# Longer priority leads for the loads, and stores issued from ACT's queue, in a hybrid gMLP, SSD and PEER block on one core

## The chip, the core and the metric

The kernel runs on one core of a Trainium2 chip. The metric is device time in microseconds (us) from launch to end; the table below gives the runs of the kernel before the change and one profiled execution of it. A core has five engines with an instruction queue each, which run in parallel and each in order: TensorE (PE, matmuls; its weight loads are listed as PEld), VectorE (DVE), ScalarE (ACT), GpSimd (POOL) and SyncE (SP, which here does nothing but issue DMA transfers). An instruction that waits for a semaphore holds everything behind it on its own queue.

## The reference

One block over 1024 tokens of width 1024, all in float32. It has three parts.

```python
uv, z, xbc, dt_raw, gate_pre = split(x @ w_in)          # 10272 columns
ya = gmlp_branch(uv, ...) @ gm_w_out                    # gelu, layer norm, causal mixing in chunks of 128
yb = ssd_branch(z, xbc, dt_raw, ...) @ ssd_w_out        # conv, chunked state-space scan, 32 heads
merged = gates[0] * ya + gates[1] * yb
x1 = layer_norm(ALPHA * x + merged @ w_o)
# PEER: 8 heads, each picks 16 of 16384 experts per token
q = x1 @ w_q;  s1, s2 = q . k1, q . k2;  top-16 of each, then top-16 of their sums -> experts, gates
act = gelu(sum_d u[experts] * x1);  ch = sum_k gates * act * v[experts]
ple = sigmoid(x1 @ ple_w_gate + b) * (p @ ple_w_proj)
out = layer_norm(ALPHA * x1 + ch + ple)
```

## The kernel before

The tokens are cut into three groups of 256, 384 and 384 (`GROUPS`). For each, `front` runs the dense layers of the block: gMLP (`w_v`, `w_u`, then eight pairs of `w_g` and `gm_w_out`), SSD (16 pairs of heads `j`, each with `make_x`, `core_g`, `core`), the merge, `w_o`, and the query and key products (`w_q`, `kT`). The experts of the first two groups are gathered row by row from DRAM by POOL (`gather`, 4 KB per partition), multiplied on DVE (`row`, L822) and PE (`pacc`, L864). This side work is spread over the later groups' `front` by the loop at the end of the kernel. The third group instead multiplies by all 16384 experts: `dense_scores` and `dense_gates` prepare 48 of 128 score tiles (`s_d`) and the gate table (`g_d`) in DRAM, then `dense` runs 16 steps of 8 pieces. A piece of a step either loads its score tile (`ew<-s`) or makes it on PE (`ew<-mm` by ACT), multiplies it with a gate tile (`gte`, one load of 12 by 128 stretches per partition for four pieces) and splits it in two; `po` then takes 768 by 3 matmuls of it, and `eacc` adds `po` into the result. Six of the 16 steps load their pieces; they are called the loading steps here.

Every weight goes through `weights`: a load into `raw` (4 buffers), a cast to `whi` on ACT (3 buffers), and the rest `wlo` on DVE (3 buffers). PE multiplies high by high, high by low and low by high.

A scheduler orders the program. It takes instructions by priority, which is the order in which they were written unless `tc.high_priority(offset=n)` moves one n places ahead, and it places a load once its buffer is free in its own account of the program. The queues are then fixed: SP issues its DMAs in that order, whether or not a later one could go. Before the change SP issues every load of weights and activations and nearly every store; ACT issues none. The stores wait on SP for what they store.

The lines that matter: L144 issues `raw`, L146 and L147 make `whi` and `wlo`; L348 stores `m0`, L440 loads the state of the group before into `pv`, L452 stores the new state, L486 stores `yacc`; L571 stores `x1` for the gathers; L590 loads `kT`; L917 and L952 store the scores `s` and gates `g`; L975 and L980 load `gte` and `ew`; L1013 is the `eacc` addition.

Of the kernel before, what the change touches and what calls it, by code (L numbers as in the profile page):

```python
# [8 lines left out]
F32 = mybir.dt.float32  # L9
# [13 lines left out]
NG = len(GROUPS)  # L23
# [3 lines left out]
NCOL = 32  # L27
# [13 lines left out]
CST = 300  # L41
AHEAD_W = (20, 20)
AHEAD_G = 40
LEAD = 50
# [34 lines left out]
def block_kernel(ctx, tc, a, out):  # L79
# [135 lines left out]
    def front(gi):  # L215
        NB, mode = GROUPS[gi]
# [23 lines left out]
        with tc.tile_pool(name="ga", bufs=1, side=side_) as ga, \  # L240
# [17 lines left out]
            with tc.tile_pool(name="sd", bufs=1, side=side_) as sd:  # L258
# [50 lines left out]
                for c in range(NB):  # L309
                    DMA.dma_start(arow[:, c, :], act[c * NCOL:(c + 1) * NCOL, :])  # L310

# [11 lines left out]
            for g in range(8):  # L323
# [15 lines left out]
                yield 1.2 * unit  # L339
            m0 = []  # L340
            for j in range(8):
                pg = channel_major(a["w_g"][j], xh, xl)
                sg = gb.tile([128, T], F32, name="sg", tag="t1", bufs=3)
                A.activation(sg, pg, AF.Sigmoid, bias=bgate[:, j:j + 1])
                py = channel_major(a["gm_w_out"][j], gh, gl)
                V.tensor_mul(sg, sg, py)
                m0.append(dram.tile([128, T], F32, name=f"m0_{gi}_{j}"))
                DMA.dma_start(m0[j], sg)  # L348
                beside()
                yield 2 * unit  # L350

        for _ in previous:
# [5 lines left out]
        yacc = []  # L358
# [5 lines left out]
        with tc.tile_pool(name="sa", bufs=1, side=side_) as sa, tc.tile_pool(name="sb", bufs=2, side=side_) as sb:  # L364
# [17 lines left out]

            bT, cT, xs, zs, arows, btok, cbm = [{} for _ in range(7)]

# [6 lines left out]
            def make_x(j):  # L391
                arows[j] = sb.tile([128, 2, T], F32, name="arow_t")
                DMA.dma_start(arows[j], bass.AP(tensor=arow.tensor, offset=arow.offset + 2 * j * T,
                                                ap=[[0, 128], [T, 2], [1, T]]))
                xs[j] = conv(channel_major(a["w_xbc"][j], xh, xl), j, "xs")
                yield unit
                zp = channel_major(a["w_z"][j], xh, xl)
                zs[j] = sb.tile([128, T], F32, name="zs")
                A.activation(zs[j], zp, AF.Silu)
                yield unit  # L400
# [14 lines left out]
            def core(j):  # L415
# [22 lines left out]
                pv = sa.tile([128, NB, 2, 64], F32, name="pv")  # L438
                if gi > 0:
                    DMA.dma_start(pv[:, 0], state_d[gi - 1, j])  # L440

                for c in range(NB if gi < NG - 1 else NB - 1):
                    if c + gi == 0:
                        A.copy(pv[:, 1], pst_[:, 0])
                        continue
                    for h in range(2):
                        V.scalar_tensor_tensor(pv[:, (c + 1) % NB, h], pv[:, c, h],
                                               cdec[:, c, 2 * j + h:2 * j + h + 1], pst_[:, c, h],
                                               op0=OP.mult, op1=OP.add)
                if gi < NG - 1:  # L450
                    state_d[gi, j] = dram.tile([128, 2, 64], F32, name=f"state_{gi}_{j}")
                    DMA.dma_start(state_d[gi, j], pv[:, 0])  # L452
                V.tensor_mul(dec, dec, cbm[g].unsqueeze(1).to_broadcast([128, 2, NB, 128]))
# [4 lines left out]
                for c in range(NB):  # L458
                    for h in range(2):
                        o = py[h * 64:h * 64 + 64, c, :]  # L460
                        PE.matmul(o, lhsT=xdt[:, c, h, :], rhs=dec[:, h, c, :], start=True, stop=(c + gi == 0),
                                  tile_position=(0, h * 64))
                        if c + gi > 0:
                            PE.matmul(o, lhsT=pv[:, c, h, :], rhs=ce[:, h, c * 128:c * 128 + 128],
                                      start=False, stop=True, tile_position=(0, h * 64))
# [4 lines left out]
                sq = rrow if j == 0 else sa.tile([128, T], F32, name="sq")  # L470
                A.activation(sq, y, AF.Square)
                if j > 0:
                    V.tensor_add(rrow, rrow, sq)
# [6 lines left out]
            def first_half():  # L480
                for j in range(8):
                    p = channel_major(a["ssd_w_out"][j, 0], yfh, yfl)
                    o = sb.tile([128, T], F32, name="yo")
                    A.copy(o, p)
                    yacc.append(dram.tile([128, T], F32, name=f"yacc_{gi}_{j}"))
                    DMA.dma_start(yacc[j], o)  # L486
                    yield unit
# [73 lines left out]
        with tc.tile_pool(name="qa", bufs=1, side=side_) as qa, tc.tile_pool(name="qb", bufs=2, side=side_) as qb:  # L561

            for c in range(NB):
                mv = qb.tile([128, 2], F32, name="mv")
                V.bn_aggr(mv, st[:, c])
                rs = rstd_of(mv[:, 1:2], 1, qb)
                V.scalar_tensor_tensor(x1[:, c], x1[:, c], mv[:, 0:1], lg, op0=OP.subtract, op1=OP.mult)
                V.scalar_tensor_tensor(x1[:, c], x1[:, c], rs, lb, op0=OP.mult, op1=OP.add)
                if mode == "gather":
                    x1_d[gi, c] = dram.tile([128, 1024], F32, name=f"x1_{gi}_{c}")  # L570
                    DMA.dma_start(x1_d[gi, c], x1[:, c])  # L571
            for u in range(4):
                for cc, p in token_major([a["ple_w_proj"][u]], ph, pl, 2):
                    A.copy(proj[:, cc, u * 256:u * 256 + 256], p)
                yield 0.5 * unit
            for c in range(NB):
                for k4 in range(2):
                    pt = pst.tile([128, 4, 128], F32, name="mt", tag="mt")
                    for k in range(4):
                        kk = 4 * k4 + k  # L580
                        PE.transpose(pt[:, k, :], x1[:, c, kk * 128:kk * 128 + 128], ident)
                    sl = (slice(None), slice(4 * k4, 4 * k4 + 4), slice(c * 128, c * 128 + 128))
                    split(xh[sl], xl[sl], pt)
# [3 lines left out]
            for u in range(16):  # L587
                p = channel_major(a["w_q"][u], xh, xl)
                kT = qb.tile([128, 128], F32, name="kT", bufs=3)
                DMA.dma_start(kT, a["kT"][:, u, :])  # L590
                qT = qb.tile([128, T], F32, name="qT")
# [318 lines left out]
    def dense_scores(gi, xh, xl, pool):  # L910

        for i2 in range(sum(AHEAD)):
# [3 lines left out]
            s_d[gi, i2] = dram.tile([128, xh.shape[2]], F32, name=f"s_{gi}_{i2}")  # L916
            DMA.dma_start(s_d[gi, i2], w)  # L917
            yield UNIT * xh.shape[2] / 512

    def dense_gates(gi, NB, pst):  # L920
        with tc.tile_pool(name="da", bufs=1) as da, tc.tile_pool(name="db", bufs=3) as db:
# [9 lines left out]
            for c in range(T // TC):  # L931
# [19 lines left out]
                for b in range(0, 128 * TC, 2048):  # L951
                    DMA.dma_start(g_d[gi][c, :, b:b + 2048], gf[:, b:b + 2048])  # L952

    def dense(gi, t0, NB, xh, xl):
        T = NB * 128
        with tc.tile_pool(name="ea", bufs=1) as ea, tc.tile_pool(name="eb", bufs=2) as eb, \
# [35 lines left out]
            for step, b in enumerate(order):  # L992
# [3 lines left out]
                for h in range(2):  # L996
# [14 lines left out]
                    for c in range(NB):  # L1011
                        o = acc[:, c, h * 512:h * 512 + 512]
                        V.tensor_add(o, o, po[c])  # L1013
                        if last:
                            V.bn_stats(st[:, c, h, :], o)
# [104 lines left out]
```

## Time and profile before

| | |
|---|---|
| median of 3 runs | 3764.52 us (3756.73 to 3765.45) |
| the profiled execution | 3774.55 us, of which 3772.9 us is the span from the first to the last instruction |
| busy, share of the span | PE 91%, PEld 78%, DVE 78%, ACT 47%, POOL 43% |
| moved by DMA | 1183.88 MB, mean 314 GB/s |
| mean granted PE clock | 0.955 of full speed |

The profiled execution is 10.0 us longer than the median of the runs. An idle figure in a row stands for the time just before the instructions named, and the name behind the arrow is what ended the wait. SP counts no busy time: its rows tell when it issued a DMA and how long that took. A load's time of flight is the time from its issue to its landing.

### The profile page before, as it was taken

The numbers are of one execution on the slowest core, as the hardware profiler recorded it, in microseconds if no ns is written. First come the engines' busy times: TensorE is split into PE (matmuls) and PEld (weight loads), VectorE is DVE, ScalarE is ACT, GpSimd is POOL, SyncE is SP. The second block draws the span as 40 slices with busy tenths as digits, with TensorE's granted clock in tenths as the row PEclk, the third lists the DMA queues.
The fourth block names the chain that finished last, engine by engine and source line by source line (L and its number), as shares of the span: only waits on it lengthen the run. The fifth ranks groups of instructions, "written<-read, shape, count | busy, mean of one in ns | idle before, by whom it ended". The sixth has DMA issues, their size and how long they took to land.

```text
span 3772.9 us, 59493 instructions
## 1 busy us (share of the span) xinstructions
PE 3437.7 (91%) x21390; PEld 2946.2 (78%) x21390; DVE 2936.8 (78%) x6823; ACT 1756.0 (47%) x2675; POOL 1606.3 (43%) x1310
## 2 busy tenths in 40 slices
PE   8898997999989988999988989998889989989988
PEld 8897996988877876888878888777667868667756
DVE  6677799898977989896688999997667766766535
ACT  6788543476843333466652334774222323322223
POOL 0000004756545354554354445443556565665540
PEclk9998998999999988999989999999999999999999
DMA  5453656989879886989888899999999999999992
GB/s 200 161 172 130 238 180 241 389 309 356 317 279 385 309 324 234 356 311 343 305 326 327 298 338 349 362 377 372 360 381 400 395 386 389 368 383 401 356 350 95
DMA packets 409159, 1183.88 MB, mean 314 GB/s; under 512 B 41120, under 2 KB 139424, under 8 KB 405792
## 3 DMA queue, kind: packets, MB, share of 16 engines
q0 software_dynamic: 187488, 682.71, 47.7%
q1 hardware_dynamic: 221376, 497.38, 36.9%
q8 instruction: 168, 2.75, 0.3%
q14 instruction: 127, 1.04, 0.1%
HBM read 1121.01 MB, written 58.92 MB: 313 GB/s over the span
## 4 chain that ended last, share of the span: by engine, by line
PE 33%; DVE 16%; DMA 13%; issue 4%; ACT 1%; POOL 1%; SPq 0%; DVEq 0%; ACTq 0%; POOLq 0%
PE mm L152 6%; PE mm L154 6%; PE mm L153 6%; PE pacc L864 4%; DVE row L822 3%; DVE wlo L147 3%; DMA ew<-s 3%; PE po L152 3%; DMA row<-in_peer_v_dram,idxT 3%; PE po L153 3%; PE po L154 3%; DMA raw<-in_peer_uT_dram 2%; PE mt L947 2%; DMA row<-in_peer_u_dram,idx 1%; DMA raw<-in_peer_vd_dram 1%
## 5 line engine op out<-in xcount | busy, mean ns | idle before, releaser
L146 ACT CAST whi<-raw 128x1024 fp32r<-128x1024 f32 (+1 forms) x676 | 701.1, 1041 | 1192.4 <-PE mm L153 612.0
L803 POOL DMA_INDIRECT row<-in_peer_u_dram,idx x640 | 811.5, 1268 | 874.9 <-PE pacc L864 254.3
L147 DVE TENSOR_TENSOR wlo<-raw,whi 128x1024 fp32r<-128x1024 f32 (+1 forms) x676 | 816.2, 1210 | 375.5 <-ACT whi L146 374.7
L154 PE MATMUL mm<-xh,wlo 128*128 128x384 f32 (+2 forms) x3160 | 1056.4, 335 | 46.7 <-DVE wlo L147 46.7
L152 PE MATMUL mm<-xh,whi 128*128 128x384 f32 (+2 forms) x3160 | 1066.3, 338 | 34.3 <-ACT whi L146 25.6
L803 POOL DMA_INDIRECT row<-in_peer_v_dram,idxT x640 | 780.9, 1220 | 712.0 <-PE pacc L864 232.5
L153 PE MATMUL mm<-xl,whi 128*128 128x384 f32 (+2 forms) x3160 | 1051.9, 333 | 0.6 <-DVE xl L136 0.6
L822 DVE SCALAR_TENSOR_TENSOR row<-row,x1b 128x1024 f32<-128x1024 f32 x640 | 774.6, 1217 | 64.8 <-DMA row<-in_peer_u_dram,idx 58.5
L152 PEld LDWEIGHTS mm<-xh,whi 128*128 128x128 f32 (+1 forms) x3160 | 611.2, 194 | 89.7 <-ACT whi L146 46.1
L154 PEld LDWEIGHTS mm<-xh,wlo 128*128 128x128 f32 (+1 forms) x3160 | 609.8, 193 | 66.4 <-DVE wlo L147 55.0
L153 PEld LDWEIGHTS mm<-xl,whi 128*128 128x128 f32 (+1 forms) x3160 | 610.5, 193 | 12.2 <-issue 6.1
L864 PE MATMUL pacc<-row,zw 128*32 128x512 f32 x2560 | 316.9, 614 | 37.0 <-DMA row<-in_peer_v_dram,idxT 36.8
L152 PE MATMUL po<-whi,ewh 128*128 128x512 f32 x768 | 316.0, 411 | 32.2 <-DVE eacc L1013 32.2
L153 PE MATMUL po<-wlo,ewh 128*128 128x512 f32 x768 | 311.0, 405 | 14.4 <-DVE wlo L147 14.3
L154 PE MATMUL po<-whi,ewl 128*128 128x512 f32 x768 | 309.9, 404 | 0.0
L152 PEld LDWEIGHTS po<-whi,ewh 128*128 128x128 f32 x768 | 148.3, 193 | 104.6 <-DVE eacc L1013 36.1
L864 PEld LDWEIGHTS pacc<-row,zw 128*32 128x32 f32 x2560 | 67.9, 111 | 180.6 <-issue 131.1
L135 ACT CAST ewh<-ew 128x384 fp32r<-128x384 f32 x128 | 65.6, 514 | 296.7 <-DVE ew L985 230.1
L818 POOL DMA_DIRECT2D x1b<-x x5 | 3.0, 601 | 446.4 <-DMA x<-x 446.4
L153 PEld LDWEIGHTS po<-wlo,ewh 128*128 128x128 f32 x768 | 148.5, 193 | 51.0 <-DVE wlo L147 16.8
L154 PEld LDWEIGHTS po<-whi,ewl 128*128 128x128 f32 x768 | 148.1, 193 | 40.9 <-issue 5.0
L153 PE MATMUL mm<-wlo,xh 128*128 128x256 f32 x512 | 147.8, 289 | 11.4 <-DVE wlo L147 11.4
(272 smaller groups left out, 5603.8 us busy)
## 6 DMA issues: line engine op xcount, KB each, us to landing
raw<-in_peer_uT_dram SPq DMA_DIRECT2D x128, 512.0 KB, 8.0
raw<-in_peer_vd_dram SPq DMA_DIRECT2D x128, 512.0 KB, 6.8
raw<-in_w_xbc_dram SPq DMA_DIRECT2D x96, 512.0 KB, 5.9
raw<-in_w_g_dram SPq DMA_DIRECT2D x48, 512.0 KB, 6.7
raw<-in_w_z_dram SPq DMA_DIRECT2D x48, 512.0 KB, 5.4
raw<-in_ssd_w_out_dram SPq DMA_DIRECT2D x48, 512.0 KB, 5.3
raw<-in_w_q_dram SPq DMA_DIRECT2D x48, 512.0 KB, 4.7
g<-gt SPq DMA_DIRECT2D x24, 1024.0 KB, 7.5
```

The lines of the kernel that those rows point to most:

```text
L135: A.copy(hi, src)
L146: A.copy(hi, raw)
L147: V.tensor_sub(lo, raw, hi.bitcast(F32))
L152: PE.matmul(p, lhsT=lh, rhs=rh, start=start, stop=False, skip_group_check=skip)
L153: PE.matmul(p, lhsT=lh, rhs=rl, start=False, stop=False, skip_group_check=skip)
L154: PE.matmul(p, lhsT=ll, rhs=rh, start=False, stop=stop, skip_group_check=skip)
L803: g = POOL.indirect_dma_start(out=t, out_offset=None, in_=a[tab], in_offset=bass.IndirectOffsetOnAxis(ap=ix, axis=0))
L818: POOL.dma_start(x1, x1_d[gi, c])
L822: u = V.scalar_tensor_tensor(t, t, 1.0, x1, op0=OP.mult, op1=OP.mult, accum_out=act[:, k:k + 1])
L864: return PE.matmul(pacc[q * 32:q * 32 + 32, h * 512:h * 512 + 512], lhsT=zws[z][:, q, r % 4, :], rhs=ts[q][:, h * 512:h * 512 + 512], star ...
L947: PE.matmul(p[:, i, :], lhsT=o1, rhs=o2, start=True, stop=True)
```

## The change

Priorities: a weight's load goes from 20 to 150 places ahead (`AHEAD_W[0]`), the dense group's `gte` and `ew` loads from 40 to 300 (`AHEAD_G`), and the `eacc` addition, which had no offset, gets 60 (`AHEAD_E`). The `kT` load becomes one of two tiles and gets the weights' 150. Stores: `arow`, `m0`, `state`, `yacc`, `x1`, `s` and `g` go to ACT's queue, 157 DMAs in all; `m0` is issued one turn later than its product, `state` after the square of `y`, `x1` after the `ple_w_proj` products. The state of the group before is loaded into a tile of its own (`p0`, 2 buffers) in `make_x`, ahead of its use. Buffers stay as they are, apart from `p0` and `kT`.

```diff
-AHEAD_W = (20, 20)
-AHEAD_G = 40
+AHEAD_W = (150, 20)
+AHEAD_G, AHEAD_E = 300, 60
...
-                    DMA.dma_start(arow[:, c, :], act[c * NCOL:(c + 1) * NCOL, :])
+                    A.dma_start(arow[:, c, :], act[c * NCOL:(c + 1) * NCOL, :])
...
                 A.activation(sg, pg, AF.Sigmoid, bias=bgate[:, j:j + 1])
+                if late:
+                    A.dma_start(*late.pop())
                 py = channel_major(a["gm_w_out"][j], gh, gl)
                 V.tensor_mul(sg, sg, py)
                 m0.append(dram.tile([128, T], F32, name=f"m0_{gi}_{j}"))
-                DMA.dma_start(m0[j], sg)
+                late.append((m0[j], sg))
...
+                if gi > 0:
+                    pvs[j] = sb.tile([128, 2, 64], F32, name="p0")
+                    DMA.dma_start(pvs[j], state_d[gi - 1, j])
                 xs[j] = conv(channel_major(a["w_xbc"][j], xh, xl), j, "xs")
...
-                if gi > 0:
-                    DMA.dma_start(pv[:, 0], state_d[gi - 1, j])
+                p0 = pvs.pop(j, None)
...
-                    DMA.dma_start(state_d[gi, j], pv[:, 0])
...
                 A.activation(sq, y, AF.Square)
+                if gi < NG - 1:
+                    A.dma_start(state_d[gi, j], pv[:, 0])
...
-                    DMA.dma_start(yacc[j], o)
+                    A.dma_start(yacc[j], o)
...
-                    DMA.dma_start(x1_d[gi, c], x1[:, c])
+                    A.dma_start(x1_d[gi, c], x1[:, c])
...
-                kT = qb.tile([128, 128], F32, name="kT", bufs=3)
-                DMA.dma_start(kT, a["kT"][:, u, :])
+                if u % 2 == 0:
+                    k2 = qb.tile([128, 2, 128], F32, name="kT")
+                    with tc.high_priority(offset=AHEAD_W[0]):
+                        DMA.dma_start(k2, a["kT"][:, u:u + 2, :])
...
-            DMA.dma_start(s_d[gi, i2], w)
+            A.dma_start(s_d[gi, i2], w)
...
-                    DMA.dma_start(g_d[gi][c, :, b:b + 2048], gf[:, b:b + 2048])
+                    A.dma_start(g_d[gi][c, :, b:b + 2048], gf[:, b:b + 2048])
...
-                        V.tensor_add(o, o, po[c])
+                        with tc.high_priority(offset=AHEAD_E):
+                            V.tensor_add(o, o, po[c])
```

What the scheduler makes of it is seen in the queues. First SP at the end of the score and gate stage (`raw<-in_peer_uT` are the weights, `s` and `sah` the score stores, `eacc<-base` and `gte` the first loads of `dense`), before:

```order
L144 DMA raw<-in_peer_uT_dram 128x1024 x2
L917 DMA s_44_28235<-sah 128x384
L962 DMA eacc<-base_23083 128x1024
L917 DMA s_45_28284<-sah 128x384
L962 DMA eacc<-base_23083 128x1024 x2
L144 DMA raw<-in_peer_uT_dram 128x1024
L917 DMA s_46_28324<-sah 128x384
L144 DMA raw<-in_peer_uT_dram 128x1024 x2
L917 DMA s_47_28364<-sah 128x384
L144 DMA raw<-in_peer_uT_dram 128x1024 x2
L975 DMA gte<-g_24888 128x12x128 x2
```

The same place of SP after the change:

```order
L144 DMA raw<-in_peer_uT_dram 128x1024 x3
L761 DMA sel_2_24683<-sT 128x384
L144 DMA raw<-in_peer_uT_dram 128x1024
L938 DMA sT<-sel_2_24683 128x3x128
L144 DMA raw<-in_peer_uT_dram 128x1024 x28
L144 DMA raw<-in_peer_vd_dram 128x1024
L985 DMA gte<-g_24872 128x12x128 x2
L972 DMA eacc<-base_23067 128x1024 x3
```

The stores are gone from between the weights, which now stand in an unbroken row of 28, and the `eacc` loads have moved behind the first `gte`.

Second, SP in a loading step of `dense`, the one that loads the score tiles 8 to 15 (`ew<-s_2_8` to `s_2_15`; the number behind a tile's name is that of its creation), before:

```order
L980 DMA ew_34321<-s_2_10_23979 128x384
L144 DMA raw_34487<-in_peer_vd_dram 128x1024
L975 DMA gte_34420<-g_2_24888 128x12x128
L980 DMA ew_34370<-s_2_11_24137 128x384
L980 DMA ew_34422<-s_2_12_24191 128x384
L144 DMA raw_34536<-in_peer_vd_dram 128x1024
L980 DMA ew_34475<-s_2_13_24258 128x384
L975 DMA gte_34622<-g_2_24888 128x12x128
L980 DMA ew_34516<-s_2_14_24322 128x384
```

and after:

```order
L990 DMA ew_34305<-s_2_10_23963 128x384
L144 DMA raw_34471<-in_peer_vd_dram 128x1024
L985 DMA gte_34404<-g_2_24872 128x12x128
L990 DMA ew_34354<-s_2_11_24121 128x384
L144 DMA raw_34520<-in_peer_vd_dram 128x1024
L990 DMA ew_34406<-s_2_12_24175 128x384
L990 DMA ew_34459<-s_2_13_24242 128x384
L990 DMA ew_34500<-s_2_14_24306 128x384
L985 DMA gte_34606<-g_2_24872 128x12x128
```

The first `gte` still stands straight in front of the score tile 11; what moved is a weight by one place and the second `gte` by one.

Third, DVE in the same step (`ew<-ew,gte` are the products with the gate tile, `wlo` the weights' rest, `eacc` the additions, `row` the side work), before:

```order
L136 TENSOR_TENSOR ewl_34426<-ew_34422,ewh_34425 128x384
L147 TENSOR_TENSOR wlo_34448<-raw_34446,whi_34447 128x1024
L985 TENSOR_TENSOR ew_34475<-ew_34475,gte_34420 128x384
L822 SCALAR_TENSOR_TENSOR row_34328,act_31481<-row_34328,x1b_31479 128x1024
L1013 TENSOR_TENSOR eacc_28386<-eacc_28386,po_34195 128x512
L1013 TENSOR_TENSOR eacc_28386<-eacc_28386,po_34196 128x512
L985 TENSOR_TENSOR ew_34516<-ew_34516,gte_34420 128x384
L822 SCALAR_TENSOR_TENSOR row_34365,act_31481<-row_34365,x1b_31479 128x1024
L1013 TENSOR_TENSOR eacc_28386<-eacc_28386,po_34197 128x512
```

and after:

```order
L136 TENSOR_TENSOR ewl_34410<-ew_34406,ewh_34409 128x384
L995 TENSOR_TENSOR ew_34459<-ew_34459,gte_34404 128x384
L147 TENSOR_TENSOR wlo_34432<-raw_34430,whi_34431 128x1024
L1024 TENSOR_TENSOR eacc_28370<-eacc_28370,po_34179 128x512
L832 SCALAR_TENSOR_TENSOR row_34300,act_31465<-row_34300,x1b_31463 128x1024
L995 TENSOR_TENSOR ew_34500<-ew_34500,gte_34404 128x384
L832 SCALAR_TENSOR_TENSOR row_34312,act_31465<-row_34312,x1b_31463 128x1024
L1024 TENSOR_TENSOR eacc_28370<-eacc_28370,po_34180 128x512
L1024 TENSOR_TENSOR eacc_28370<-eacc_28370,po_34181 128x512
```

The product of score tile 13 (`ew_34475` before, `ew_34459` after) now stands ahead of the `wlo` it followed. The first addition follows that `wlo` at once, where a product and a side row stood between; between the first and the second addition there are now three rows where there was none.

## Rows read from the trace of the kernel before

**Rows 1.** The page, parts 1 and 2: busy time, the span in 40 slices.
```profile
PE 3437.7 (91%) x21390; PEld 2946.2 (78%) x21390; DVE 2936.8 (78%) x6823; ACT 1756.0 (47%) x2675; POOL 1606.3 (43%) x1310
...
GB/s 200 161 172 130 238 180 241 389 309 356 317 279 385 309 324 234 356 311 343 305 326 327 298 338 349 362 377 372 360 381 400 395 386 389 368 383 401 356 350 95
```

**Rows 2.** Windows by stage: stretch, length, each engine's busy time, clock, DMA share, GB/s.
```profile
520.00:1370.00 850.00, 779.72 (x5091) 702.18 (x5090) 742.89 (x1788) 420.45 (x631) 425.88 (x317) 0.96 0.86 315
1370.00:2352.00 982.00, 892.28 (x5677) 781.22 (x5675) 848.72 (x2200) 457.89 (x684) 467.70 (x381) 0.95 0.87 318
2352.00:2620.00 268.00, 243.71 (x1563) 205.37 (x1564) 247.70 (x804) 187.72 (x335) 114.53 (x103) 0.99 0.97 372
2620.00:3773.00 1153.00, 1049.42 (x5356) 805.15 (x5354) 720.94 (x1115) 327.32 (x437) 596.00 (x501) 0.95 0.94 355
```

**Rows 3.** What PE waited for over the span: total us, times, longest.
```profile
PE mm L152 <- ACT whi L146: 39.5, 29, 8.4
PE pacc L864 <- DMA row<-in_peer_v_dram,idxT: 36.8, 13, 8.4
PE po L152 <- DVE eacc L1013: 32.2, 7, 13.5
...
PE po L153 <- DVE wlo L147: 14.3, 5, 5.2
...
PE mm L152 <- ACT sah L915: 6.7, 1, 6.7
PE mt L947 <- ACT o L941: 5.7, 8, 1.1
PE mt L271 <- ACT dtw L268: 5.5, 1, 5.5
...
PE mm L786 <- ACT ew L983: 3.6, 1, 3.6
```

**Rows 4.** What SP waited for over the span, the stores' lines.
```profile
SPq L917 <- ACT sah L915: 92.0, 30, 8.3
...
SPq L348 <- DVE sg L346: 45.6, 19, 5.9
```

**Rows 5.** Timeline at the last head pair of group two: start, length, instruction, idle before.
```profile
1059.68 0.33 SPq L440 DMA_DIRECT2D pv<-state  x1
...
1067.00 0.28 DVE L447 SCALAR_TENSOR_TENSOR pv<-pv,cdec,mt 128x64 f32<-128x64 f32 x1 [6.32 <-DMA pv<-state]
...
1070.25 0.66 PE L461 MATMUL mt<-dec,xdt 128*64 128x128 f32 x2 [10.65 <-DVE dec L453]
```

**Rows 6.** What DVE waited for: the state loads.
```profile
DVE pv L447 <- DMA pv<-state: 7.9, 2, 6.3
```

**Rows 7.** Timeline of SP at the first query weights of group two.
```profile
1197.86 5.11 SPq L571 DMA_DIRECT2D x<-x  x3
1203.29 0.94 SPq L144 DMA_DIRECT2D raw<-in_w_q_dram  x2
```

**Rows 8.** Timeline at 1214 us: PE behind that load.
```profile
1213.60 1.04 ACT L146 CAST whi<-raw 128x1024 fp32r<-128x1024 f32 x1 [5.87 <-DMA raw<-in_w_q_dram]
...
1215.91 0.48 PE L581 MATMUL mt<-ident,x 128*128 128x128 f32 x1 [7.71 <-DVE xl L136]
```

**Rows 9.** Timeline at the end of the score stage.
```profile
2604.60 0.38 SPq L144 DMA_DIRECT2D raw<-in_peer_uT_dram  x1
...
2615.31 1.04 ACT L146 CAST whi<-raw 128x1024 fp32r<-128x1024 f32 x1 [8.77 <-DMA raw<-in_peer_uT_dram]
```

**Rows 10.** Timeline of SP in the loading step of tiles 8 to 15.
```profile
3360.65 0.37 SPq L975 DMA_DIRECT2D gte<-g  x1
3362.37 13.39 SPq L980 DMA_DIRECT2D ew<-s  x2
```

**Rows 11.** Timeline of DVE in the same step.
```profile
3387.12 1.13 DVE L985 TENSOR_TENSOR ew<-ew,gte 128x384 f32<-128x384 f32 x2 [14.70 <-DMA ew<-s]
```

**Rows 12.** Groups on ACT: one of the lines that load a table of functions.
```profile
L426 ACT ACT_TABLE_LOAD x46 | 59.0, 1283 | 0.8
```

More of the change, by code (lines that the diff above doesn't have):

```diff
@@ L339, in front @@
                 yield 1.2 * unit
-            m0 = []
+            m0, late = [], []
             for j in range(8):
@@ L347, in front @@
                 m0.append(dram.tile([128, T], F32, name=f"m0_{gi}_{j}"))
-                DMA.dma_start(m0[j], sg)
+                late.append((m0[j], sg))
                 beside()
                 yield 2 * unit
+            A.dma_start(*late.pop())
         for _ in previous:
@@ L381, in conv @@
                 return xc
-            bT, cT, xs, zs, arows, btok, cbm = [{} for _ in range(7)]
+            bT, cT, xs, zs, arows, btok, cbm, pvs = [{} for _ in range(8)]
             def make_bc(g):
@@ L446, in core @@
                     for h in range(2):
-                        V.scalar_tensor_tensor(pv[:, (c + 1) % NB, h], pv[:, c, h],
+                        V.scalar_tensor_tensor(pv[:, (c + 1) % NB, h], (pv[:, c] if c else p0)[:, h],
                                                cdec[:, c, 2 * j + h:2 * j + h + 1], pst_[:, c, h],
@@ L463, in core @@
                         if c + gi > 0:
-                            PE.matmul(o, lhsT=pv[:, c, h, :], rhs=ce[:, h, c * 128:c * 128 + 128],
+                            PE.matmul(o, lhsT=(pv[:, c] if c else p0)[:, h, :], rhs=ce[:, h, c * 128:c * 128 + 128],
                                       start=False, stop=True, tile_position=(0, h * 64))
@@ L568, in front @@
                 V.scalar_tensor_tensor(x1[:, c], x1[:, c], rs, lb, op0=OP.mult, op1=OP.add)
-                if mode == "gather":
-                    x1_d[gi, c] = dram.tile([128, 1024], F32, name=f"x1_{gi}_{c}")
-                    DMA.dma_start(x1_d[gi, c], x1[:, c])
             for u in range(4):
@@ L575, in front @@
                 yield 0.5 * unit
+            if mode == "gather":
+                for c in range(NB):
+                    x1_d[gi, c] = dram.tile([128, 1024], F32, name=f"x1_{gi}_{c}")
+                    A.dma_start(x1_d[gi, c], x1[:, c])
             for c in range(NB):
@@ L588, in front @@
                 p = channel_major(a["w_q"][u], xh, xl)
-                kT = qb.tile([128, 128], F32, name="kT", bufs=3)
-                DMA.dma_start(kT, a["kT"][:, u, :])
+                if u % 2 == 0:
+                    k2 = qb.tile([128, 2, 128], F32, name="kT")
+                    with tc.high_priority(offset=AHEAD_W[0]):
+                        DMA.dma_start(k2, a["kT"][:, u:u + 2, :])
+                kT = k2[:, u % 2]
                 qT = qb.tile([128, T], F32, name="qT")
```

## The prediction

> **What bounds the kernel now.** I read the page's busy times first. PE is busy 3437.7 us of the span of 3772.9 [rows 1], so PE is the bound and it stood still for 335 us in all. A change of loads and stores can only take from that idle time and from the clock: the mean granted clock of 0.955 (the table) means 0.045 x 3773 = 170 us spent at less than full speed, about 0.5 us for each idle us. I use that as the clock's share: an idle us that goes is worth between 1 and 1.5 us.
>
> Then the windows by stage. In the middle front (520 to 2352) PE and DVE are both near 90% busy (742.89 of 850 and 848.72 of 982 for DVE) and the DMA moves 315 to 318 GB/s. In the score and gate stage (2352 to 2620) DVE is busy 247.70 of 268 us: DVE is the bound there. In `dense` (2620 to 3773) PE is the bound, at 1049.42 of 1153 us, so the idle time that can be had there is 104 us [rows 2]. The slices of `dense`, the last twelve of part 2 without the very last, move 379 GB/s on average and 401 at most [rows 1].
>
> Last, the waits of PE. The largest are `whi` of ACT (39.5 us), the gathered rows `row` (36.8), the `eacc` addition (32.2), and `wlo` (14.3) [rows 3]. The gathers are POOL's and are not touched. A wait on `whi` can be a late load, a late ACT or a late store ahead of the load on SP, so I followed each gap back to its root in the timeline. What SP itself waited for shows how long stores hold it: 92.0 us in all for the scores, 45.6 us in 19 waits at `m0` [rows 4].
>
> **The change part by part.** *The state of the group before.* `pv<-state` is issued at 1059.68, DVE waits 6.32 us for it, and PE has a gap of 10.65 us behind the chain `pv`, `dec` [rows 5]. The two such waits of DVE sum to 7.9 us [rows 6]. Loaded in `make_x`, a head pair of work earlier, it is there in time. Only the waiting for the load goes, not the remainder of the gap, so I take 7.9 us: 6.3 here and 1.6 in the other group.
>
> *The first query weights.* SP spends 5.11 us in the three `x1` stores and only then issues the first `w_q` loads, at 1203.29 [rows 7]; ACT waits 5.87 us for such a load and PE 7.71 us [rows 8]. With the stores on ACT and the loads 150 places ahead the 5.11 us go; the rest (7.71 - 5.11 = 2.6) I leave, since four `raw` buffers still hold the loads back. 5.1 us.
>
> *The weights at the end of the scores.* The load of `peer_uT` issued at 2604.60, between score stores, makes ACT wait 8.77 us at 2615.31 [rows 9], and PE 6.7 us behind `sah` [rows 3]. After the change these weights stand in an unbroken row on SP. 6.7 us.
>
> Together 7.9 + 5.1 + 6.7 = 19.7 us of PE idle.
>
> *The loads of `dense`.* These have the longest new leads, 300 places, but the order of SP in a loading step differs only by neighbours that change places. What delays there is still in place: a `gte` is issued at 3360.65, the two `ew` behind it take SP 13.39 us to issue [rows 10], and DVE waits 14.70 us for the tile [rows 11]. The buffers, not the priorities, decide where these stand, and the buffers are the same. I take 0. From below: the same stall 1 us worse in each of six loading steps, 6 us; from above: all PE waits on `wlo` and `eacc`, 14.3 + 32.2 = 46.5 us [rows 3], which is rival B.
>
> *The offset of `eacc`.* On DVE the first addition moves ahead of two rows and the second behind three, so one comes earlier and one later. I take 0 of its 32.2 us [rows 3].
>
> *The price on ACT.* 157 DMA issues move to ACT. One costs SP 0.33 to 0.38 us where nothing holds it [rows 5, 9]; no row shows one on ACT, and I take the same: 157 x 0.33 = 51.8 us. The new order holds 8 table loads fewer on ACT, at 1283 ns [rows 12]: 10.3 us back. So 41.5 us more for ACT, which is busy 1756.0 us [rows 1] and has room. What of it reaches PE: PE waited for ACT 39.5 + 6.7 + 5.7 + 5.5 + 3.6 = 61.0 us [rows 3], 3.5% of ACT's busy time, part of it loads. 3.5% of 41.5 is 1.4 us, the lower end; if every issue stood in PE's way it would be 41.5 us, the upper end. The nearest row is the lower one, since ACT is idle more than half of the time; I take 4 us, because the stores come in the stages where ACT is fullest. The cover is ACT's idle time; gone, it is rival D.
>
> *The stores off SP.* SP waits less, 92.0 + 45.6 us for the two largest [rows 4], but this pays only where a load behind them was late, and those places are counted above. *kT* in pairs and the `arow` stores: no PE gap led to them, 0.
>
> [...]
>
> **The sum.** 19.7 - 4 = 15.7 us of idle, with the clock's share between 15.7 and 23.5; I take 20. 3774.55 - 20 = 3754.5 for the profiled execution, and as that is 10.0 us above the median of the runs, 3744.5, put down as 3744. The likeliest case's own range: 23.5 + 7 us from an ACT that costs nothing, so 30 better than the median before would be 3734; on the other side an ACT price of 12 us leaves about 8, 3757. So 3734 to 3757.
>
> **The rivals.** *B, the load stalls of `dense` go too.* For it: the leads grow most there, and the waits of DVE for the score tiles put `eacc` and `wlo` late. Against it: the order of the queue hardly moves, and the slow issue of `ew` stands right behind the same `gte` [rows 10]. Price: 46.5 us of idle [rows 3], with the clock 70; but a `dense` that moves the same bytes at the best rate of a slice, 401 instead of 379 GB/s, would save at most 11 slices x 94.3 us (a fortieth of the span) x (1 - 379/401) = 57 us [rows 1]. 3744.5 - 57 = 3688. [...]
>
> *C, it does not do what it says: no change.* For it: the front is bound by PE and DVE together [rows 2], so a load that comes sooner meets a DVE that isn't free; and an ACT price of 20 us, halfway to its upper end of 41.5, cancels the 19.7. Time: the median before, about 3764.
>
> *D, slower: the `m0` wait moves from SP to ACT.* The store of `m0` now stands on ACT behind the next sigmoid and waits for DVE's product. SP waited there 45.6 us in 19 waits, 5.9 at most [rows 4]. Now `whi` of the next weights queues behind it on ACT, and PE behind `whi`. It decides once DVE lags by more than one product of PE, as the store is issued one turn later than its product. For it: DVE is 87% busy in the middle stages [rows 2]. Against it: the waits that SP saw are for the same turn, and a turn of two products is longer than 5.9 us. Price: all 45.6 us on PE, so 45.6 - 20 = 25.6 slower: 3790.
>
> **How the numbers follow.** Chances: the forecast 0.42, B 0.20, C 0.20, D 0.18. 0.3% is 11.3 us, about what a measurement of this kernel can tell from no change, so faster is below 3753.2 and slower above 3775.8. Faster: B's 0.20 and 0.37 of the forecast's 0.42 (the rest ends at 3753 to 3757), 0.57. Same: 0.05 + 0.19 of C = 0.24. Slower: D's 0.18 and 0.01 of C = 0.19. The range takes in B down to 3684 (57 us and 4 of spread) and cuts D at 3784, which leaves the further half of D, some 0.1, and the tail below B, outside.
>
> **What the profile after would show.** Right: the 10.65 us gap at the last head pair is shorter and the wait of DVE for `pv<-state` gone; no ACT wait of 5.87 us at the first query weights and none of 8.77 us at the end of the scores; the wait for `ew<-s` of 14.70 us still there. B would show the latter gone, `eacc` out of PE's waits and slices of `dense` near 401 GB/s. C would show the three gaps closed and others of the same sum opened, on DVE or ACT. D would show ACT's queue waiting for DVE at the `m0` store, and PE's wait for `whi` in the front grown beyond 39.5 us. The forecast is wrong in its main step if `dense`, from the first `eacc` load to the end, changes by more than 15 us in either direction.

## The result, and the profile after

The changed kernel took 3790.3 us (median of 5 runs, 3783.12 to 3794.16), the kernel before 3764.52 (median of 5 runs beside them): a ratio of 1.0068, 95% interval 1.0051 to 1.0086. It is slower by 26 us where the forecast said 20 us faster, and its time lies above the stated range. It is also the time of rival D, but for another reason, as will be seen.

The page of the changed kernel, part 1, answers to [rows 1]:

```profile
PE 3454.0 (91%) x21390; PEld 2959.2 (78%) x21390; DVE 2939.8 (78%) x6823; ACT 1746.0 (46%) x2667; POOL 1600.7 (42%) x1310
```

The span is 3792.5 us, 19.6 more than before. PE's idle time is 3792.5 - 3454.0 = 338.5 us, only 3.3 more. The other 16.3 us are in PE's busy time with the same 21390 matmuls: they ran longer, and the mean granted clock fell from 0.955 to 0.949.

To see where, both traces are cut at the same points of PE's work (its 960th, 3840th, 7200th, 13200th, 15300th and last matmul, those into `pacc` not counted, since the side work floats). The stretches between are called group 0, group 1, group 2, the scores with the start of `dense`, and the rest of `dense`. The windows of before; the second row is a piece of the first, between the 2040th and the 2460th matmul:

```profile
131.20:536.70 405.50, 369.04 (x2882) 350.73 (x2881) 308.82 (x759) 288.73 (x485) 1.24 (x2) 0.94 0.52 175
284.90:345.70 60.80, 54.88 (x422) 50.97 (x422) 47.00 (x105) 55.19 (x102) 0.00 (x0) 0.92 0.43 145
536.70:1170.70 634.00, 581.23 (x3683) 525.61 (x3682) 553.49 (x1188) 348.04 (x525) 330.72 (x238) 0.96 0.84 311
1170.70:2342.70 1172.00, 1066.40 (x6897) 935.39 (x6897) 1017.13 (x2765) 519.62 (x775) 557.79 (x456) 0.95 0.88 321
2342.70:2799.40 456.70, 417.58 (x2469) 342.78 (x2469) 378.97 (x1018) 247.78 (x418) 217.59 (x188) 0.98 0.98 373
2799.40:3757.30 957.90, 884.08 (x4507) 674.50 (x4505) 589.68 (x910) 267.16 (x355) 498.01 (x420) 0.96 0.94 356
```

and the same work after:

```profile
131.80:553.30 421.50, 380.32 (x2883) 360.09 (x2882) 309.74 (x763) 290.51 (x485) 1.24 (x2) 0.91 0.50 168
292.60:364.20 71.60, 60.27 (x422) 55.61 (x422) 48.30 (x108) 61.27 (x109) 0.00 (x0) 0.86 0.38 126
553.30:1181.20 627.90, 583.57 (x3683) 530.76 (x3682) 551.59 (x1183) 338.59 (x516) 314.22 (x238) 0.95 0.85 314
1181.20:2350.00 1168.80, 1060.39 (x6898) 928.10 (x6897) 1018.17 (x2768) 519.39 (x775) 562.10 (x457) 0.95 0.88 322
2350.00:2821.40 471.40, 424.76 (x2470) 348.09 (x2469) 385.04 (x1021) 246.81 (x420) 222.92 (x191) 0.95 0.95 365
2821.40:3776.90 955.50, 884.93 (x4507) 674.58 (x4505) 586.68 (x903) 265.90 (x353) 499.34 (x417) 0.95 0.94 354
```

Group 0 loses 16.0 us, group 1 gains 6.1, group 2 gains 3.2, the end of the scores with the start of `dense` loses 14.7, the rest of `dense` gains 2.4; with 0.6 at the front that is the 19.6. In group 0 the loss is 4.7 us more idle time of PE and 11.3 us more busy time, in the scores with the start of `dense` 7.5 and 7.2. The piece shown of group 0 alone loses 10.8, and there ACT is busy 55.19 of 60.8 us before (91%), where it is 71% over the stretch of group 0 and 47% over the span.

ACT's timeline in that piece (start, length, instruction). Before:

```profile
330.56 1.28 ACT L426 ACT_TABLE_LOAD   x1
331.86 0.63 ACT L426 ACTIVATE ce<-arow_t 128x512 f32<-128x512 f32 x1
...
335.06 0.64 ACT L424 ACTIVATE dec<-dec 128x512 f32<-128x512 f32 x1
335.59 0.59 ACT L376 ACTIVATE cT<-xin,c_convb,c_convw 128x256 f32<-128x256 f32 x1
336.08 1.99 ACT L146 CAST whi<-raw 128x1024 fp32r<-128x1024 f32 x2
338.09 1.28 ACT L380 ACT_TABLE_LOAD   x1
```

and after:

```profile
346.18 1.28 ACT L432 ACT_TABLE_LOAD   x1
347.48 0.63 ACT L432 ACTIVATE ce<-arow_t 128x512 f32<-128x512 f32 x1
348.13 1.28 ACT L383 ACT_TABLE_LOAD   x1
...
351.57 1.28 ACT L430 ACT_TABLE_LOAD   x1
352.86 0.63 ACT L430 ACTIVATE dec<-dec 128x512 f32<-128x512 f32 x1
353.51 1.28 ACT L383 ACT_TABLE_LOAD   x1
...
355.12 1.03 ACT L146 CAST whi<-raw 128x1024 fp32r<-128x1024 f32 x1
```

Before, no table load stands between the exponentials `ce` and `dec`, and the casts `whi` stand ahead of the next one, at 338.09. After, two stand between them, at 348.13 and 351.57, and a third behind `dec`, at 353.51, each of 1.28 us, and the next `whi` comes behind it all, at 355.12. DVE's product `dec` needs ACT's `dec` and ends at 354.21. PE in the same place after:

```profile
350.36 0.28 PE L154 MATMUL mm<-xh,wlo 128*128 128x256 f32 x1
...
354.36 0.62 PE L465 MATMUL mt<-dec,xdt 128*64 128x128 f32 x6 [3.27 <-DVE dec L457]
356.20 0.58 PE L152 MATMUL mm<-xh,whi 128*128 128x256 f32 x1 [1.22 <-ACT whi L146]
...
358.79 0.41 PE L152 MATMUL mm<-xh,whi 128*128 128x256 f32 x1
```

PE has a gap of 3.27 us ahead of the products with `dec` and one of 1.22 us ahead of those with `whi`, and behind them a matmul of 128x256 takes 0.41 us where it took 0.28.

At the start of `dense`, the timeline after (several engines), in place of [rows 9]:

```profile
2652.24 1.10 ACT L958 COPY gt<-mt 128x512 f32<-128x512 f32 x1 [0.62 <-PE mt L957]
2653.38 0.81 ACTq L962 DMA_DIRECT2D g<-gt  x2
2660.93 0.87 ACT L993 ACTIVATE ew<-mm 128x384 f32<-128x384 f32 x2 [7.59 <-DMA g<-gt]
2661.09 1.41 SPq L985 DMA_DIRECT2D gte<-g  x2
2661.48 0.69 PE L152 MATMUL mm<-xh,whi 128*128 128x384 f32 x1 [7.42 <-ACT ew L993]
...
2678.33 1.03 DVE L995 TENSOR_TENSOR ew<-ew,gte 128x384 f32<-128x384 f32 x2 [12.92 <-DMA gte<-g]
...
2681.29 0.69 PE L152 MATMUL mm<-xh,whi 128*128 128x384 f32 x1 [8.92 <-ACT ew L993]
```

The last score tile starts on ACT at 2573.6 (2616.3 before) and the last gate copy at 2652.2 (2586.0 before). The two streams end in the opposite order; `dense` now waits for the gate table, first for its stores, then for the load of its first tile: gaps of 7.42 and 8.92 us in place of the 6.7 of before [rows 3].

The two places in the front that the forecast named, the last head pair of group 1 and the first query weights, against 10.65 us [rows 5] and 7.71 us [rows 8]; the second lies behind the 7200th matmul, in the stretch of group 2:

```profile
1079.97 0.70 PE L465 MATMUL mt<-dec,xdt 128*64 128x128 f32 x4 [6.17 <-DVE dec L457]
...
1220.83 1.26 PE L588 MATMUL mt<-ident,x 128*128 128x128 f32 x8 [2.23 <-DVE xl L136]
```

The loading step of [rows 10, 11] has kept its slow issue behind a `gte` and its wait, in SP's and DVE's timelines:

```profile
3379.96 0.37 SPq L985 DMA_DIRECT2D gte<-g  x1
3382.34 9.80 SPq L990 DMA_DIRECT2D ew<-s  x1
3393.59 5.27 SPq L990 DMA_DIRECT2D ew<-s  x3
...
3407.82 0.56 DVE L995 TENSOR_TENSOR ew<-ew,gte 128x384 f32<-128x384 f32 x1 [14.27 <-DMA ew<-s]
```

### The profile page after: what moved, and what is told of

Its sections match the earlier page's. It is cut to its first block, busy times and chain, and to the rows that moved or that the text cites. A ratio compares the mean times of both kernels' runs of the same rounds, so it can differ in the third digit from the quotient of the medians.

```text
span 3792.5 us, 59307 instructions
## 1 busy us (share of the span) xinstructions
PE 3454.0 (91%) x21390; PEld 2959.2 (78%) x21390; DVE 2939.8 (78%) x6823; ACT 1746.0 (46%) x2667; POOL 1600.7 (42%) x1310
## 4 chain that ended last, share of the span: by engine, by line
PE 59%; DVE 17%; DMA 14%; issue 5%; ACT 4%; POOL 1%; SPq 0%; ACTq 0%; DVEq 0%; POOLq 0%
PE mm L152 13%; PE mm L154 13%; PE mm L153 12%; PE pacc L874 5%; DVE row L832 3%; DMA row<-in_peer_v_dram,idxT 3%; PE po L152 3%; PE po L153 3%; PE po L154 3%; DVE wlo L147 3%; DMA ew<-s 3%; PE mt L957 2%; DMA row<-in_peer_u_dram,idx 1%; POOL row L813 1%; DMA raw<-in_peer_vd_dram 1%
## 5 line engine op out<-in xcount | busy, mean ns | idle before, releaser
L957 PE MATMUL mt<-o,o 128*128 128x128 f32 x768 | 146.2, 303 | 18.6 <-ACT o L951 7.0
```

Of the source, the lines that this page charges most:

```text
L957: PE.matmul(p[:, i, :], lhsT=o1, rhs=o2, start=True, stop=True)
```

## The experiments

Each ratio is to runs of the kernel before in the same job. The experiments ran on four chips; on one of them, called chip B here (e1 to e4 and e9 to e12), the kernel before took 3786 to 3788 us, on the others 3762.5 to 3763.4. Stretches are those of the windows above.

**e1 to e4: halves of the change.** Stores only; all but the stores (their lines back to the form of before); the gate table's stores only; the front's stores only. Of e3 the edit is

```diff
-                    DMA.dma_start(g_d[gi][c, :, b:b + 2048], gf[:, b:b + 2048])
+                    A.dma_start(g_d[gi][c, :, b:b + 2048], gf[:, b:b + 2048])
```

> The kernel before with only the stores moved to ACT's queue (m0, state and x1 at their new places); loads, eacc and the load of the state as before. Theory O (the stores make the scheduler order ACT and DVE in another way, at the first head pairs of group 0 and between scores and gate table, and that costs): 3785 to 3800 us, above 3764 by what the changed kernel is or a little more, since the gain at pv and w_q is missing. Theory L (the longer leads of the loads cost, the stores are free): 3764. Theory D (m0's wait holds ACT): 3790, with ACT waiting some 45 us ahead of the m0 stores, against 6.5 us in the profile of the changed kernel.

> The changed kernel with all its stores back on SP, at their old places; the longer leads, eacc's offset, p0 and kT in pairs stay. O: faster than before, 3750 to 3758 (pv and w_q gaps shorter, the gate table done ahead of the scores as before). L: 3785 to 3795. D: 3745 to 3755.

> The kernel before with only the 24 stores of the gate table on ACT's queue. In the program the 48th score tile then comes after 73 of 96 gate copies instead of after all 96. O: the first score product of the dense group waits for the table, PE gaps of some 7 and 9 us there, and 3772 to 3780 in all. L and D: 3764.

> The kernel before with the arow, m0, state, yacc and x1 stores on ACT, and the scores' and the gate table's stores on SP. O: group 0 loses some 15 us up to its end by smaller gaps and a lower clock, 3774 to 3782 in all, and the gate table is done ahead of the scores as before. L: 3764. D: 3790.

Measured: e1 1.0058 (1.0040 to 1.0077); e2 1.0013 (0.9997 to 1.0030); e3 0.9993 (0.9978 to 1.0008); e4 1.0027 (1.0012 to 1.0043). The stores carry the loss in group 0: its stretch is 421.1 and 416.9 us in e1 and e4, 401.7 and 403.4 in e2 and e3. Theory L, by which the leads cost and the stores are free, falls. The gain that theory O expected in the total of e2 and the loss that it expected in that of e3 did not come, though e3 has its two gaps at the start of `dense`, 7.71 and 9.00 us. In e2 the last head pair of group 1 is quicker (80.2 us between the 6300th and 6700th matmul, 85.8 in e3), but between the 5300th and 5900th it is slower (114.7 against 109.1), and the gap at the query weights, with `x1`'s stores on SP, stays at 6.70 us.

**e5 to e8: the state stores.** Which front store it is was found in the order: with `state` alone on ACT's queue, ACT's and DVE's rows in group 0 change from about the 40th weight on; writing the store at its new place but leaving it on SP changes no row. e5 has that one edit, e6 the changed kernel without it, e7 and e8 repeat the changed kernel and that of before for their profiles.

```diff
-                    DMA.dma_start(state_d[gi, j], pv[:, 0])
...
+                    A.dma_start(state_d[gi, j], pv[:, 0])
```

> The kernel before with only the 32 stores of the scan state on ACT's queue, 16 of them in group 0. Without any other edit this reorders ACT and DVE between the 40th and the 120th weight of group 0, and with the same number of table loads. Theory O, as it now stands: it is this order that costs group 0: the stretch from PE's 960th to its 3840th matmul (the pacc products not counted) takes 415 to 422 us where the kernels with this store on SP have 402 to 405, and the ratio to before is 1.002 to 1.005. Rival I (only the issues cost, 0.33 us each, in place): 16 issues in group 0, 5 us at most there, ratio 1.000 to 1.002. Rival M (m0's stores are the cause in the front): ratio 1.000, group 0 as before.

> The changed kernel with the stores of the scan state back on SP. O: group 0's stretch back at 402 to 405 us; ratio to before some 0.004 lower than that of the changed kernel in the same job, 1.001 to 1.004, the rest being the score and gate stage. I: 0.001 lower. M: no difference to the changed kernel.

> The changed kernel again, beside the others of this job: ratio to before 1.005 to 1.009; group 0's stretch 421 us. This is for the comparison by stage with the next one on the same chip; no theory differs on it.

> The kernel before again, for a profile on the chip of this job. Group 0's stretch 402 to 406 us. O expects the stretch from the 13200th to the 15300th matmul (the end of the scores and the start of dense) 10 to 15 us shorter than in the changed kernel, since the gate table is ready ahead of the last scores; if the stretch is as long here as in the kernels with those stores on SP on the second chip (473 to 477 us), the loss in that stage was the chip's and not the change's.

Measured: e5 1.0041 (1.0025 to 1.0057), e6 1.0012 (0.9999 to 1.0025), e7 1.0052 (1.0039 to 1.0065). Group 0: e8 406.1 us, e5 416.6, e6 404.1, e7 417.2. The window of e8, group 0, and those of e5, group 0 and its piece:

```profile
131.10:537.20 406.10, 369.17 (x2882) 350.88 (x2882) 309.00 (x760) 288.73 (x485) 1.24 (x2) 0.94 0.54 175
131.20:547.80 416.60, 376.10 (x2883) 356.76 (x2882) 308.82 (x759) 290.24 (x485) 1.24 (x2) 0.93 0.53 170
287.80:359.30 71.50, 60.16 (x422) 55.43 (x421) 48.37 (x108) 61.26 (x109) 0.00 (x0) 0.86 0.40 127
```

This is the piece of the changed kernel to within 0.1 us. It holds 5 DMA issues, 1.7 us at 0.33 each, and costs 10.8 us, so rival I falls. Nor does the store's own wait hold ACT: ahead of the 16 state stores of group 0 it stands idle for 0.7 us in all. The piece holds 13 table loads instead of 11, but over the whole of group 0 there are 47 in e8 and in e5, and ACT is busy 288.7 and 290.2 us: the work is the same, its order is not. M falls too: e6 keeps m0's late stores. The stretch of scores and `dense` is 454.2 us in e8 and 469.3 and 470.3 in e7 and e6, so that loss is the change's.

**e9 to e12: the other loss, and what is left of the gains.** e9 has the stores of `s` and `g` on ACT; e10 is the changed kernel with `state`, `s` and `g` on SP; e11 takes from e10 the leads of `dense` (`AHEAD_G = 40`, no offset at `eacc`); e12 is the kernel before with `p0`, kT in pairs and the `x1`, `yacc` and `arow` stores on ACT.

```diff
-            DMA.dma_start(s_d[gi, i2], w)
+            A.dma_start(s_d[gi, i2], w)
```

> The kernel before with only the stores of the scores and of the gate table (72) on ACT's queue. In the program the last score tile then comes after 65 of 96 gate copies, instead of after all 96. Theory O: the gates end alone, PE idles more there and dense waits for the table: the stretch from PE's 13200th to its 15300th matmul 10 to 15 us longer, ratio 1.002 to 1.004, group 0 unchanged. Rival C (the 15 us of that stretch come from the longer leads, W, E and G, not from these stores): ratio 1.000 and the stretch as before.

> The changed kernel with the stores of the scan state, the scores and the gate table back on SP; the other stores stay on ACT, and the leads, p0, kT in pairs and the eacc offset stay. O: both losses gone, the gains of group 1 (8 to 12 us) left: ratio 0.995 to 0.999. C: 1.000 to 1.002, as the changed kernel without the state stores (1.0012).

> The kernel of e10 with the dense group's leads and the eacc offset back as before (40, and none). If these are worth what the forecast took, nothing, its ratio is that of e10 within 0.0015. If they gain in dense: 0.002 or more above e10. If the eacc offset harms the side work in dense: 0.002 or more below e10.

> The kernel before with p0, kT in pairs and the x1, yacc and arow stores on ACT alone; weights' lead 20, m0, state, score and gate stores on SP. The forecast's pv and w_q terms alone: 7.9 + 5.1 = 13 us, ratio 0.996 to 0.998, and in group 1's stretch (3840th to 7200th matmul) 8 to 13 us less. O has nothing against that, unless the new order between the 160th and 240th weight costs: then 1.000, with a gap at the head pairs of group 1.

Measured: e9 1.0014 (0.9998 to 1.0030), e10 0.9998 (0.9986 to 1.0010), e11 1.0004 (0.9991 to 1.0017), e12 0.9997 (0.9982 to 1.0012). The stretch of scores and `dense` in e9 and in e12, where these stores are on SP:

```profile
2348.00:2830.30 482.30, 428.76 (x2470) 352.28 (x2469) 386.49 (x1020) 247.63 (x420) 221.53 (x190) 0.95 0.93 355
2340.50:2811.70 471.20, 425.75 (x2470) 346.47 (x2469) 382.59 (x1021) 249.46 (x420) 219.62 (x190) 0.97 0.97 362
```

With e1 (479.0 us) and e4 (472.8) beside them, the stores cost 6 to 11 us there on chip B, but the total of e9 is not clear of no change. Of all twenty profiles, the seven with the gate table's stores on ACT have the two gaps at the start of `dense` (7.3 to 7.7 and 8.4 to 9.3 us); the others have none there above 6.8 us. e10 takes back the stores behind both losses and still did not come out ahead: group 0 is back at 403.3 us, but the stretch of scores and `dense` is 482.0 us. e10 and e11 do not differ, so the leads of `dense` are worth nothing that can be measured. e12, which the forecast's terms would put at 0.996 to 0.998, shows no gain.

**e13 to e16: the weights' lead, and room on ACT.** e13 is `AHEAD_W = (150, 20)` alone. e14 takes 32 multiply-adds of group 0, the convolution's first step, from ACT to POOL, which is busy 1.24 us in that stretch of before; e15 does that in the changed kernel; e16 is the kernel before, for a profile.

```diff
-                A.activation(xc, xin[:, 3:], AF.Identity, bias=convb[:, u:u + 1], scale=convw[:, u, 3:4])
+                if gi == 0:
+                    POOL.tensor_scalar(xc, xin[:, 3:], convw[:, u, 3:4], convb[:, u:u + 1], op0=OP.mult, op1=OP.add)
+                else:
+                    A.activation(xc, xin[:, 3:], AF.Identity, bias=convb[:, u:u + 1], scale=convw[:, u, 3:4])
```

> The kernel before with only the weights' load lead of 150 instead of 20. Theory W (the loads of uT now stand in one row ahead of the first gate tile and the first products of dense wait for it): 6 to 9 us more between PE's 14600th and 15300th matmul than in the kernel before of this job, ratio 1.001 to 1.003. Forecast's term: the 6.7 us gap at the end of the scores gone, ratio 0.997 to 0.999. Rival (chance of the chip): no difference in that stretch, 1.000.

> The kernel before with the first step of the convolution (one multiply-add over 256 tokens per channel block, 32 in group 0) on POOL instead of ACT, in group 0 alone. Theory A (ACT is the bound at the head pairs of group 0, busy 78 of 85 and 55 of 61 us there): group 0's stretch (960th to 3840th matmul) 8 to 20 us shorter than 406, ratio 0.995 to 0.998. Rival (ACT has room, as the forecast took it, and the order alone made the loss): 1.000, or worse where POOL's step is slow.

> The changed kernel with the same step of group 0 on POOL. A: group 0's stretch falls from 417 to 421 us to 405 or less, and the ratio from 1.005 to 1.007 to 1.000 to 1.003. Rival: as the changed kernel, 1.005 to 1.007.

> The kernel before, for a profile on the chip of this job. All theories: group 0's stretch 402 to 406 us; the stretch from the 13200th to the 15300th matmul 454 to 457 us if it is the first chip, some 472 if the second.

Measured: e13 1.0002 (0.9988 to 1.0016), e14 0.9967 (0.9955 to 0.9978), e15 0.9999 (0.9986 to 1.0012). e14's windows of group 0 and its piece:

```profile
131.10:520.50 389.40, 364.43 (x2883) 346.12 (x2882) 309.19 (x759) 265.33 (x450) 27.97 (x31) 0.96 0.55 182
274.60:331.40 56.80, 54.29 (x423) 50.13 (x422) 45.93 (x103) 50.26 (x92) 6.44 (x8) 0.94 0.47 149
```

Against e16's 403.0 us group 0 is 13.6 us shorter, though POOL needs 0.88 to 1.05 us, means by tile, for a step that took ACT 0.59 to 0.60. Part of this is order again: group 0 has 41 table loads in e14 and 47 in e16, 7.7 of the 22.9 us that ACT is relieved of. In e15, with the state stores on ACT and 47 table loads as in the changed kernel, it is 394.2, against 417.2 in e7 (on another chip). So ACT's load was a limit of that stage. In e13 the gap at the last scores falls from 5.50 us (e16) to 3.76, and the gap behind the first product with a gate tile grows from 2.09 to 4.98: the wait moved.

**e17 and e18: do the front's parts gain on top.** e17 is e12 with POOL's step. e18 is the changed kernel with POOL's step, the three kinds of stores on SP and the weights' lead at 20.

> The kernel of e12 (p0, kT in pairs, the x1, yacc and arow stores on ACT) with the convolution step of group 0 on POOL. If the two gaps are worth what the forecast took (13 us, less what the order gives back): ratio 0.993 to 0.995. If the shorter gaps only move the wait, as e12's 0.9997 says: 0.996 to 0.998, as e14.

> The changed kernel with the convolution step of group 0 on POOL, the stores of the scan state, scores and gate table on SP, and the weights' lead at 20. If m0's late store shortens group 1 by the 8 to 12 us that the changed kernel showed there: ratio 0.993 to 0.995. If not: 0.996 to 0.998.

Measured: e17 0.9925 (0.9904 to 0.9947), 3736.97 us against 3763.43; e18 0.9939 (0.9919 to 0.9959). Both beat the kernel before and the changed one. e17's windows of group 0 and group 1:

```profile
130.90:520.80 389.90, 362.26 (x2881) 344.12 (x2881) 310.08 (x765) 264.86 (x449) 28.28 (x31) 0.96 0.56 182
520.80:1147.80 627.00, 583.71 (x3682) 529.85 (x3681) 551.31 (x1180) 331.83 (x512) 305.64 (x239) 0.95 0.86 314
```

Group 1 is 627.0 us against 638.4 in e14 and 632.8 in e16, which ran on another chip: 6 to 11 us for what e17 has beyond e14. Between the 6300th and the 6700th matmul, where the last head pair lies, it is 78.3 us against 85.4, which speaks for `p0`; no run has `p0` alone. The `x1` stores have no share in group 1's gain by the query weights, which lie in the stretch of group 2, and that takes 1167.9 us in e17 and 1166.1 in e14. On chip B e12 has the same 78.6 us at the last head pair (85.6 in e9), but 112.7 us between the 5300th and the 5900th matmul (107.7 in e9). Why, and why its total shows no gain, stays open.

## Why the prediction was wrong

The step that failed is the price on ACT: "What of it reaches PE: [...] 3.5% of 41.5 is 1.4 us [...]; I take 4 us". It spread a mean over the span on stages that have other limits, and ACT is busy 91% in the head pairs of group 0 shown above. And it priced only the issues and the table loads saved, when the larger cost was a new order of ACT: the rows of order that the forecast looked at were SP's and DVE's. In group 0 the state stores alone cost 10.5 us (e5 less e8, in profiles of one job), and e14 and e15 confirm that ACT's load is the limit there. Of eleven profiles with this store on SP and ACT's work unmoved, group 0 takes 401.7 to 406.1 us in all; of five with it on ACT, 416.6 to 421.5. It is not `whi` that PE waits for longer: in group 0 that wait falls from 10.1 us (e8) to 6.4 (e5), and over the span from 39.5 to 22.5 in the changed kernel. What grows in group 0 is the wait for `dec`, from 6.4 to 9.5 us, for `pv`, from 0.4 to 3.1, for `xs`, from none to 2.6, and for `wlo`, from 2.4 to 3.9, all made by ACT or from what ACT makes.

The count was off too, without weight for the result: the trace has 165 DMA issues on ACT, not 157 (48 of `s`, 32 of `state`, 24 each of `m0`, `yacc` and `g`, 8 of `arow`, 5 of `x1`), 54.5 us at 0.33 each.

The second failed step is "The weights at the end of the scores. [...] 6.7 us". That gap is gone, but the gate table, its stores on ACT, now comes last: 14.7 us lost where 6.7 were to be gained. With both stores on ACT the last score comes after 65 of 96 gate copies, with `g` alone after 73 (e3), before the change after all 96. Nor would the weights' lead have earned the 6.7 us by itself: in e13 the wait moved.

No run in which stores alone moved gained anything clear (e1 1.0058, e3 0.9993, e4 1.0027, e5 1.0041, e9 1.0014). But the gap at the query weights is 2.25 us or less in all eleven profiles with the `x1` stores on ACT, and 6.70 to 7.86 us in the nine with them on SP, so the wait on SP's queue was real. The loss itself is not in the forecast.

The clock's share, "an idle us that goes is worth between 1 and 1.5 us", fits the gaps that went in e14 and not those that came in the changed kernel. In group 0 e14 has 9.5 us less idle time than e16 and 4.1 us less busy time, 1.4 us for each idle us. In the changed kernel 4.7 us more idle (gaps of 36.5 and 41.2 us summed over group 0) came with 11.3 us more busy time. The 170 us of the forecast are also not the time spent at less than full speed: the clock records in the profile of before put 340 us of the span at 0.5 of full speed.

What held, as gaps: the state load (10.65 to 6.17 and 8.80 to 7.87 us, 5.4 us for 7.9 forecast; 4.3 us from e8 to e7) and the query weights (7.71 to 2.23, 5.5 for 5.1). The gap at the last head pair is 3.80 to 8.51 us in the ten profiles with `p0` and 8.97 to 10.65 in the ten without. Group 1 gains 6.1 us in the first profile and 12.4 in e7 against e8. But the stretch of group 2, which holds the gap at the query weights, takes 1165.5 us in e7 and 1166.4 in e8: closing that gap shows no gain there. The leads in `dense` gave nothing to speak of, as forecast (-2.4 us from the 15300th matmul to the end), so rival B falls.

Rival C fails by the interval, though e12, with both gaps shortened and without the two losses, comes out as C said. Rival D named the right sign and by chance the time: in the changed kernel ACT stood idle ahead of all `m0` issues together 6.5 us, not 45.6, PE's wait for `whi` did not grow, and with m0's stores left as they are, e6 takes back most of the loss. What stays open is the cost of the weights' lead at the start of `dense` on chip B, where that stretch is longer with it (e2, e10 and e11: 476.7 to 482.0 us) than without (e4 and e12: 472.8 and 471.2); e13, with that lead alone, took 1.0002 of the kernel before on another chip.

## What to carry to other kernels

Price an instruction that moves to another queue by the busy share of that engine in the stage where it lands, not by its mean (here 91% in the piece of group 0 and 47% over the span), and look at the new order of that engine itself: in e5 the move of the state stores, 16 in group 0 at 0.33 us each, came with another order of ACT and DVE and 10.5 us more there. Where a stage has a full engine, take work off it before tuning the loads: POOL's slower step gained 12 us (e14), and the gain of the front's parts showed in a total only beside it (e17, not e12, which ran on another chip). And look for a closed gap in the time of its stretch: in e13 one gap fell from 5.50 to 3.76 us and another grew from 2.09 to 4.98.

## What the runs showed of the hardware

In the piece of group 0 (2040th to 2460th matmul) the gaps summed to 5.9 us before and to 11.3 after, 5.4 more. With the same 422 matmuls PE's busy time rose by 5.4 us as well, from 54.88 to 60.27, and the mean granted clock fell from 0.92 to 0.86. Near the gaps of 3.27 and 1.22 us, which end at 354.36 and 356.20, the clock records in the profile after stand at 0.5 of full speed from 355.6 to 362.5 us, and the 128x256 matmul took 0.41 us there where it took 0.28 at 350.36, with the records at full speed. Over the span 389 us stand at 0.5 after, 340 before. The same program, the kernel before, took 0.6% longer on chip B (3786 to 3788 us) than on the three others of the experiments (3762.5 to 3763.4).
